# Output projection of a transformer layer as seven half-size products, with weight sums made in DRAM during attention

## The chip, the cores and the metric

The kernel runs on one core of one Trainium2 chip. The core has five engines that work from queues of their own: TensorE (PE: matmuls and transposes), VectorE (DVE), ScalarE (ACT), GpSimd (POOL) and SyncE (SP, which here only issues transfers). POOL issues transfers too, among them the ones that add to what stands at their destination. The metric is the device time of one execution in microseconds (us), the median of several.

## The reference

One layer of a streaming encoder for 512 tokens of 1024 channels, all in fp32:

```python
h = rms_norm(x, mix_norm_pre)
xa, ga, q, k, v, f_logit, g_a, g_b = split(h @ w_in)
y_a = gelu(ga) * rg_lru(causal_dwconv(xa))          # recurrent branch
y_b = forgetting_attention(q, k, v, f_logit)        # 16 heads
merged = sigmoid(g_a) * (y_a @ w_proj_a) + sigmoid(g_b) * (y_b @ w_proj_b)
mix_out = merged @ w_out                            # the output projection, 512x1024 by 1024x1024
x = x + rms_norm(mix_out, mix_norm_post)
h = rms_norm(x, ffn_norm_pre)
up = causal_dwconv(h @ w_up)                        # 1024 -> 6144
x = x + rms_norm((gelu(gate) * val) @ w_down, ffn_norm_post)
```

The change concerns `merged @ w_out` and what stands on both sides of it.

## The kernel before

**Arithmetic.** Every fp32 matrix is parted into a high and a low piece of the type fp32r, and a product is three matmuls: high by high, high by low, low by high. A weight block arrives by an SP transfer in a buffer `raw`; ACT casts it to the high piece `wh` (L172) and DVE subtracts to get the low piece `wl` (L175). Class `Split` does this, in buffers that rotate, four of each kind. The list `order` names all weight blocks in the order of use, and `unit(name, ahead)` stages the next blocks of the list before it hands out the one wanted.

**The order of the work.** A scheduler in the framework fixes one instruction order for each engine when the kernel is built; on the chip each engine goes through its order and waits on semaphores. So an instruction that waits holds up all behind it on its engine.

**Stages around the change.** After the recurrent branch come the projections for q, k and the gate `ma` with the attention of one head pair behind the next (about 280 to 440 us). Then for each of 8 output blocks e a gate projection `mb` and the projection `pb` of the attention's output `yb`; DVE multiplies gate and projection (L820), POOL adds the other branch (L821), ACT and DVE part the result into `mh` and `ml`, [128, 8, 512] each: the merged activations, channels on partitions.

**The output projection** (`out_matmuls` L832 to L840, `out_phase` L978 to L990). The 512 tokens are four tiles of 128. Phase 0 makes tiles 0 and 1, phase 1 tiles 2 and 3, each with all eight blocks of 128 rows of `w_out`, so `w_out` is read and parted twice (16 loads). A phase is 8 blocks by 2 tiles by 2 halves of 512 columns by 3 matmuls, 96 in all, 192 for both. In the last two blocks of a phase the matmuls are sorted by token tile.

**The norm of a tile** (`mix_norm`, L952 to L976). From the product in PSUM: ACT squares and sums (L957), DVE multiplies by the gain (L958), then a square root on ACT and a reciprocal on DVE (L233, L235), DVE adds the result to x (L965), ACT squares that (L967), a second root, DVE makes the normed tile `xn` (L973), PE transposes it (16 transposes, L257), ACT writes `h2h` and the copy `hf` (L261, L263), DVE writes `h2l` (L262). The norms of tiles 0 and 1 run during phase 1, with their transposes behind blocks 3 and 4 of that phase. The norms of tiles 2 and 3 run while the first six up-products use tokens 0 to 255 only (`first_half`).

**Sums in the background.** The down projection at the kernel's end is done with seven half-size products already; its sums of weight quarters `td` are made in DRAM by transfers that POOL issues, some of them adding (`down_sums` L124 to L142, `background` L147). `background(n, w)` lets POOL copy one element of a weight block that has just been staged (a tick) and issues n transfers behind it.

Of the kernel before, what the change touches and what calls it, by code (L numbers as in the profile page):

```python
# [8 lines left out]
F32 = mybir.dt.float32  # L9
# [7 lines left out]
P = 128  # L17
S = 512
# [45 lines left out]
def kernel(  # L64
# [54 lines left out]
    td = [[tdram.tile([P, D], F32, name=f"td{i}_{m}") for m in range(NS)] for i in range(4)]  # L119
# [4 lines left out]
    def down_sums():  # L124
# [7 lines left out]
        for m in range(NS + 3):  # L132
            if m < NS:
                for t, (i, c) in enumerate(((0, 0), (1, 1), (0, 1), (1, 0))):
                    yield put(t, m, down_block(i, c, m))
            if 0 <= m - 1 < NS:
                yield add(0, m - 1, down_block(0, 1, m - 1))
                yield add(2, m - 1, down_block(1, 1, m - 1))
            if 0 <= m - 2 < NS:
                yield add(1, m - 2, td[0][m - 2])  # L140
            if 0 <= m - 3 < NS:
                yield add(3, m - 3, td[1][m - 3])  # L142

    transfers = down_sums()
    tick = cpool.tile([P, 1], F32, name="tick")

    def background(n, w):  # L147
# [6 lines left out]
    class Split:  # L154


        def __init__(self, src, shape, name, pl=None):
# [4 lines left out]
            pl = pl or wpool  # L162
            self.raw = wpool.tile([P, n], F32, tag="raw", name=f"raw_{name}", padded_shape=[P, 1024])
# [7 lines left out]
        def hi(self):  # L171
            act.copy(self.wh, self.raw)  # L172

        def lo(self, engine):
            engine.tensor_tensor(out=self.wl, in0=self.raw, in1=self.wh.bitcast(F32), op=ALU.subtract)  # L175
# [7 lines left out]
    def rows(w, k):  # L183
        return w[k * P : (k + 1) * P, :], (D,)
# [14 lines left out]
    for ph in range(2):  # L199
        order += [(f"wo{ph}_{k}", *rows(w_out, k)) for k in range(KD)]  # L200
# [463 lines left out]
    def gate_tile(e, which):  # L664
        c = 0 if which == "ma" else KD
        pg = bank(f"{which}{e}")
        project(pg, unit(f"{which}{e}"), hh, hl)
# [4 lines left out]
    with ExitStack() as at:  # L672
# [108 lines left out]
        for p in range(KD):  # L781
            bias = prep_alloc(p)
            pq, pk = bank(f"q{p}"), bank(f"k{p}")
            project(pq, unit(f"q{p}"), hh, hl)
            if prev is not None:
                normalise(prev)
            project(pk, unit(f"k{p}"), hh, hl)
# [18 lines left out]
    h2h = h2pool.tile([P, KD, S], F32R, name="h2h")  # L806
    h2l = h2pool.tile([P, KD, S], F32R, name="h2l")
    offset(gstk, 448, "right")
    mgpool = gstk.enter_context(tc.tile_pool(name="merged", bufs=1, side="right", reuse_waits="tile"))
    mh = mgpool.tile([P, KD, S], F32R, name="mh")  # L810
    ml = mgpool.tile([P, KD, S], F32R, name="ml")
    for e in range(KD):
# [4 lines left out]
        for k in range(KD):  # L817
# [3 lines left out]
        pool.tensor_tensor(out=tg, in0=tg, in1=pa[:, e], op=ALU.add)  # L821
        act.activation(out=mh[:, e], in_=tg, func=AF.Copy, scale=0.5)
        dve.scalar_tensor_tensor(out=ml[:, e], in0=tg, scalar=0.5, in1=mh[:, e].bitcast(F32),
                                 op0=ALU.mult, op1=ALU.subtract)
# [7 lines left out]
    def out_matmuls(acc, toks, k, ah, al, wh, wl, nk, halves=(0, 1)):  # L832
        for t in toks:
            tok = slice(t * P, (t + 1) * P)
            for hf in halves:
                c = slice(512 * hf, 512 * hf + 512)
                dst = acc[t][hf]
                pe.matmul(dst, ah[:, tok], wh[:, c], start=k == 0, stop=False)  # L838
                pe.matmul(dst, ah[:, tok], wl[:, c], start=False, stop=False)
                pe.matmul(dst, al[:, tok], wh[:, c], start=False, stop=k == nk - 1)  # L840

    KH, SH = KD // 2, S // 2

    def sub(out, a, b):
        dve.tensor_tensor(out=out, in0=a, in1=b, op=ALU.subtract)  # L845

    A, B = slice(0, 512), slice(512, 1024)
    X, Y = slice(0, SH), slice(SH, S)
# [94 lines left out]
    with ExitStack() as mix:  # L943
# [8 lines left out]
        def mix_norm(t, acc):  # L952
            u = npool.tile([P, D], F32, tag="u", name=f"u{t}")
            xn = npool.tile([P, D], F32, tag="xn", name=f"xn2_{t}")
            s2 = small.tile([P, 2], F32, tag="s2", name=f"s2_mix{t}")
# [546 lines left out]
```

## Time and profile before

| what | value |
| --- | --- |
| median of three runs | 928.02 us (927.01, 928.02, 928.88) |
| the profiled execution: its own time | 926.11 us |
| the profiled execution: its span | 924.2 us |
| PE busy | 911.7 us of the span, 99% |
| output projection, first matmul to first up-product | 517.58 to 562.99 us |
| packets of all transfers | 182.29 MB |

The span runs from the first to the last instruction; the execution's own time is 1.9 us longer. In rows of the timeline the columns are start, duration, engine, line and operation with output and inputs, and in brackets the idle time before it and what ended that. In rows of the windows they are the stretch, its length, then busy time and count for PE, PE's weight loads, DVE, ACT and POOL, then the granted clock of PE, the share of the transfer engines and GB/s. In rows of the chain of waits they are start, time on the chain and the step. Rows of transfers end with the median time from issue to landing.

### The profile page before, as it was taken

The page shows a single profiled execution, that of the slowest core. Times are in us where ns is not written, and L with a number is a line of the kernel's source. Part 1 is how long each engine was busy: PE and PEld are TensorE (multiplying, and loading weights), DVE is VectorE, ACT ScalarE, POOL GpSimd, SP SyncE. Part 2 cuts the span into 40 slices and gives each one's busy share as a digit, 9 for nine tenths or more (in the row PEclk, how much of TensorE's full clock was granted, in tenths as well). Part 3 has the DMA queues.
Part 4 walks back from the last instruction along what each step waited for, and adds up shares of the span by engine and source line. Part 5 has one row for each costly group of instructions (what it writes and reads, how often), then busy time and mean ns, then how long its engine had stood idle before and what let it go on. Part 6 is the DMA issues. An engine that isn't in the chain of part 4 may idle for free.

```text
span 924.2 us, 14992 instructions
## 1 busy us (share of the span) xinstructions
PE 911.7 (99%) x5582; PEld 796.1 (86%) x5582; DVE 685.2 (74%) x1121; ACT 568.8 (62%) x982; POOL 230.6 (25%) x240
## 2 busy tenths in 40 slices
PE   8999999999999999999999999999999999999996
PEld 7988888887888888888888889999999999978885
DVE  5866369632857777777644588999999999889897
ACT  7555495433345566666423376688888888676664
POOL 4134345444242232220111000042323323100001
PEclk9999999999999999999999999999999999999998
DMA  7677589989776566553232755188898888799764
GB/s 278 216 227 208 165 207 256 270 211 253 176 229 152 160 148 157 151 150 86 69 114 91 271 182 163 34 212 235 218 238 204 234 208 211 223 372 325 240 201 142
DMA packets 76282, 182.29 MB, mean 197 GB/s; under 512 B 7281, under 2 KB 35745, under 8 KB 75826
## 3 DMA queue, kind: packets, MB, share of 16 engines
q1 hardware_dynamic: 45056, 123.13, 39.5%
q0 software_dynamic: 30864, 57.68, 30.2%
q8 instruction: 44, 0.72, 0.3%
q10 hardware_dynamic: 290, 0.53, 0.1%
q14 instruction: 28, 0.23, 0.1%
HBM read 148.59 MB, written 33.64 MB: 197 GB/s over the span
## 4 chain that ended last, share of the span: by engine, by line
PE 94%; DVE 2%; DMA 1%; issue 1%; ACT 0%; POOL 0%; SPq 0%; DVEq 0%; POOLq 0%
PE up L924 7%; PE up L922 7%; PE up L921 7%; PE dn L1225 4%; PE dn L1224 4%; PE dn L1223 4%; PE pa L223 2%; PE ga L224 2%; PE ga L223 2%; PE pa L224 2%; PE pa L222 2%; PE ga L222 2%; PE q L222 2%; PE ma L222 2%; PE wo L838 2%; PE mb L222 2%
## 5 line engine op out<-in xcount | busy, mean ns | idle before, releaser
L868 POOL DMA_DIRECT2D ml<-raw_up x41 | 35.0, 855 | 154.8 <-ACT ml L867 79.2
L1076 DVE SCALAR_TENSOR_TENSOR u<-up,cpt,u 128x511 f32<-128x511 f32 x96 | 71.2, 745 | 2.6 <-ACT u L1070 0.9
L1225 PE MATMUL dn<-wh_dn,al 128*128 128x512 f32 x168 | 65.6, 391 | 0.9 <-DVE al L845 0.8
L1224 PE MATMUL dn<-wl_dn,ah 128*128 128x512 f32 x168 | 65.4, 389 | 0.0
L1223 PE MATMUL dn<-wh_dn,ah 128*128 128x512 f32 x168 | 65.4, 389 | 0.0
L921 PE MATMUL up<-sh,th 128*128 128x256 f32 x252 | 60.4, 277 | 0.5 <-ACT x L928 0.5
L922 PE MATMUL up<-sl,th 128*128 128x256 f32 x252 | 60.2, 276 | 0.0
L175 DVE TENSOR_TENSOR wl_dn<-raw_dn,wh_dn 128x1024 fp32r<-128x1024 f32 x42 | 51.5, 1226 | 9.1 <-ACT wh_dn L172 9.1
L172 ACT CAST wh_dn<-raw_dn 128x1024 fp32r<-128x1024 f32 x42 | 44.1, 1050 | 17.5 <-issue 10.3
L845 DVE TENSOR_TENSOR tl<-t,th 128x1024 fp32r<-128x1024 f32 x42 | 51.1, 1218 | 1.3 <-ACT th L902 1.3
L1084 POOL TENSOR_TENSOR yf<-u,u 128x512 f32<-128x512 f32 x24 | 32.0, 1333 | 71.8 <-issue 47.5
L1070 ACT ACTIVATE u<-up,cpt 128x512 f32<-128x512 f32 x48 | 36.9, 778 | 19.8 <-PE up L924 11.0
L921 PEld LDWEIGHTS up<-sh,th 128*128 128x128 f32 x252 | 47.3, 188 | 0.7 <-ACT x L928 0.7
L922 PEld LDWEIGHTS up<-sl,th 128*128 128x128 f32 x252 | 47.3, 188 | 0.0
L902 ACT CAST th<-t 128x1024 fp32r<-128x1024 f32 x42 | 43.9, 1045 | 4.5 <-DVE t L845 1.8
L689 POOL DMA_DIRECT2D B<-maskf x32 | 39.1, 1628 | 27.2 <-DMA B<-cnd 24.1
L922 PE MATMUL up<-h2l,mh 128*128 128x256 f32 x168 | 40.2, 276 | 0.0
L921 PE MATMUL up<-h2h,mh 128*128 128x256 f32 x168 | 40.2, 276 | 0.0
L924 PE MATMUL up<-sh,tl 128*128 128x256 f32 x252 | 38.8, 276 | 0.0
L1225 PEld LDWEIGHTS dn<-wh_dn,al 128*128 128x128 f32 x168 | 31.5, 188 | 8.1 <-DVE al L845 1.7
L175 DVE TENSOR_TENSOR wl_pa<-raw_pa,wh_pa 128x640 fp32r<-128x640 f32 x16 | 13.1, 819 | 32.8 <-ACT wh_pa L172 32.8
L1224 PEld LDWEIGHTS dn<-wl_dn,ah 128*128 128x128 f32 x168 | 31.5, 188 | 6.6
(654 smaller groups left out, 3167.7 us busy)
## 6 DMA issues: line engine op xcount, KB each, us to landing
raw_up<-in_w_up_dram SPq DMA_DIRECT2D x48, 512.0 KB, 5.4
td<-in_w_down_dram POOLq DMA_DIRECT2D x36, 512.0 KB, 5.9
raw_dn<-td SPq DMA_DIRECT2D x24, 512.0 KB, 5.0
B<-cnd POOLq DMA_DIRECT2D x16, 640.0 KB, 4.8
ml<-raw_up POOLq DMA_DIRECT2D x20, 512.0 KB, 5.3
raw_dn<-in_w_down_dram SPq DMA_DIRECT2D x18, 512.0 KB, 3.5
raw_wo<-in_w_out_dram SPq DMA_DIRECT2D x16, 512.0 KB, 3.8
td<-td POOLq DMA_DIRECT2D x12, 512.0 KB, 10.8
```

What stands on the lines that cost most here:

```text
L172: act.copy(self.wh, self.raw)
L175: engine.tensor_tensor(out=self.wl, in0=self.raw, in1=self.wh.bitcast(F32), op=ALU.subtract)
L222: pe.matmul(dst, ah, bh, start=first, stop=False)
L845: dve.tensor_tensor(out=out, in0=a, in1=b, op=ALU.subtract)
L902: act.copy(self.th[i], self.t[i])
L921: pe.matmul(dst, wh[:, k], ah[:, k], start=first and k == 0, stop=False, skip_group_check=True)
L922: pe.matmul(dst, wh[:, k], al[:, k], start=False, stop=False, skip_group_check=True)
L924: pe.matmul(dst, wl[:, k], ah[:, k], start=False, stop=k == KH - 1, skip_group_check=True)
L1076: dve.scalar_tensor_tensor(out=c[:, s:], in0=ps[:, : S - s], scalar=col(C_CFW + 3 * e + j), in1=c[:, s:], op0=ALU.mult, op1=ALU.add)
L1223: pe.matmul(dst[t], ah[:, k, tok], wh[:, k], start=first, stop=False, skip_group_check=True)
L1224: pe.matmul(dst[t], ah[:, k, tok], wl[:, k], start=False, stop=False, skip_group_check=True)
L1225: pe.matmul(dst[t], al[:, k, tok], wh[:, k], start=False, stop=last, skip_group_check=True)
```

## The change

The output projection becomes seven products of half size. `w_out` is cut into four quarters (512 by 512), the merged activations into four quarters by channel half and token half (X: tiles 0 and 1, Y: tiles 2 and 3), and products of sums of quarters are added up. Each product is 2 steps (m = 0, 1) of 12 matmuls: 14 steps, 168 matmuls of 512 columns. The steps are in the order of products 1, 4, 5, 6, 7, 3, 2.

The sums of weight quarters `tw` are made by 16 transfers (8 that put, 8 that add), one behind a tick after each q, k and `ma` projection from p = 3 on, and after each `mb`. Six blocks (products 2, 3 and 7) are loaded and parted once more ahead: `cut` entries in the last six rounds of the `pb` loop; POOL writes their high and low pieces to DRAM, and SP reads the ready pieces back when the step's turn comes (L180), so those steps need no cast and no subtraction. The sums of activations are made in `merge` (L860): four POOL operations on 128x256, parted by ACT and DVE.

Products 1, 4 and 5 are copied out of PSUM by ACT (`hold`), and later products that share an accumulator (slots) are added by DVE (`fold`, L1013), with ACT squaring (L1017) and POOL multiplying by the gain (L1018). Tiles 0 and 1 are complete after step 9 (product 7); tiles 2 and 3 after product 2, whose last steps are sorted by tile. The table `then` sets which of hold, fold and norm comes behind which step.

The core of the diff (the same quarter sums serve the down projection, as before):

```diff
+    def quarter_sums(td, block, n):
...
+    transfers = quarter_sums(td, down_block, NS)
+    wo_transfers = quarter_sums(tw, out_block, NW)
+    PRODUCTS = (1, 4, 5, 6, 7, 3, 2)
+    WQ = {1: (0, 0), 2: (1, 0), 3: (1, 1), 4: 3, 5: 0, 6: 1, 7: 2}
+    OUT = [(n, m) for n in PRODUCTS for m in range(NW)]
...
+            self.split = isinstance(src, tuple)
+            if self.split:
+                self.wh = pl.tile([P, n], F32R, tag="wh", name=f"wh_{name}")
+                self.wl = pl.tile([P, n], F32R, tag="wl", name=f"wl_{name}")
+                for t, part in zip((self.wh, self.wl), src):
+                    nc.sync.dma_start(t.bitcast(F32), part)
+                return
...
+    AHEAD = [(n, m) for n in (2, 3, 7, 6)[: 6 // 2] for m in range(NW)]
...
-    for ph in range(2):
-        order += [(f"wo{ph}_{k}", *rows(w_out, k)) for k in range(KD)]
+        if e >= KD - len(AHEAD):
+            n, m = AHEAD[e - KD + len(AHEAD)]
+            order.append((f"cut{n}_{m}", out_quarter(n, m), (2, 512)))
+            cut[n, m] = [tdram.tile([P, D], F32, name=f"cut{n}_{m}_{x}") for x in "hl"]
+    order += [(f"wo{n}_{m}", tuple(cut[n, m]) if (n, m) in cut else out_quarter(n, m), (2, 512)) for n, m in OUT]
...
+    def merge(e, tg):
...
+        pool.tensor_tensor(out=tg, in0=tg, in1=pa[:, e], op=ALU.add)
+        parted(m2h[:, i], m2l[:, i], tg)
+        pool.tensor_tensor(out=raw[:, 0], in0=tg[:, X], in1=f[:, X], op=ALU.subtract)
+        pool.tensor_tensor(out=raw[:, 3], in0=raw[:, 0], in1=f[:, Y], op=ALU.add)
+        pool.tensor_tensor(out=raw[:, 1], in0=raw[:, 3], in1=tg[:, X], op=ALU.subtract)
+        pool.tensor_tensor(out=raw[:, 2], in0=raw[:, 3], in1=tg[:, Y], op=ALU.subtract)
+        for c, scale in ((slice(0, 2), 0.5), (slice(3, 4), -0.5), (slice(2, 3), 0.5)):
+            parted(qh[:, c, i], ql[:, c, i], raw[:, c], scale)
...
+        if f"cut{e}" in cut_at:
+            n, m = cut_at[f"cut{e}"]
+            parts = unit(f"cut{n}_{m}")
+            for t, part in zip(cut[n, m], parts):
+                nc.gpsimd.dma_start(t, part.bitcast(F32).rearrange("p a b -> p (a b)"))
...
+        def hold(t, h, ps):
+            act.copy(us[t][:, HALVES[h]], ps)
+
+        def fold(t, h, ps):
+            c = us[t][:, HALVES[h]]
+            dve.tensor_tensor(out=c, in0=ps, in1=c, op=ALU.add)
...
+            act.activation(out=xns[t][:, HALVES[h]], in_=c, func=AF.Square, accum_out=s2s[t][:, h : h + 1])
+            pool.tensor_tensor(out=c, in0=c, in1=gb[0][:, HALVES[h]], op=ALU.mult)
...
+        then = {
+            1: [lambda: (hold(2, 0, slot[1][0]), hold(3, 0, slot[1][1]))],
+            3: [lambda: (hold(0, 0, slot[4][0]), hold(1, 0, slot[4][1]))],
+            5: [lambda: (hold(0, 1, slot[5][0]), hold(1, 1, slot[5][1]))],
+            7: [lambda: (hold(2, 1, slot[1][0]), hold(3, 1, slot[1][1]))],
+            9: [lambda t=t, h=h: fold(t, h, slot[1][t]) for t in range(2) for h in (1, 0)] + [lambda: go(0)],
+            10: [lambda: go(1), lambda: go(0)],
+            11: [lambda: go(1)] + [lambda t=t: fold(2 + t, 1, slot[5][t]) for t in range(2)],
+        }
+        late = []
+        for i, (n, m) in enumerate(OUT):
+            w = unit(f"wo{n}_{m}", 3)
+            if i < len(OUT) - NW:
+                out_step(i, w)
+            else:
+                late.append((i, w))
+            for f in then.get(i, ()):
+                f()
...
+        for t in range(2):
+            for args in late:
+                out_step(*args, (t,))
+            go(t)
+        for t in range(2):
+            fold(2 + t, 0, slot[2][t])
```

What the scheduler makes of this is seen at three places.

**PE at the transposes of tiles 0 and 1.** Before, the transposes of tile 0 (`tr_f_0_*`, from the normed tile `xn2_0`) stand behind block 3 of phase 1:

```order
L838 MATMUL wo3_1_5254<-wh_wo1_3_5310,mh_4630 128x512
L839 MATMUL wo3_1_5254<-wl_wo1_3_5311,mh_4630 128x512
L840 MATMUL wo3_1_5254<-wh_wo1_3_5310,ml_4631 128x512
L257 MATMUL tr_f_0_0_5379<-ident_72,xn2_0_5256 128x64
L257 MATMUL tr_f_0_1_5380<-ident_72,xn2_0_5256 128x64
```

After them come the other transposes of tile 0, 12 matmuls of `wo`, the 16 transposes of tile 1, and 36 more matmuls of `wo` ahead of the first up-product. After the change, at the same tile (`wo2_0` and `wo2_1` are here the accumulators of product 2 for tiles 2 and 3):

```order
L1054 MATMUL wo2_0_5561<-wh_wo2_1_5476,m2h_4687 128x512
L1055 MATMUL wo2_0_5561<-wl_wo2_1_5477,m2h_4687 128x512
L1056 MATMUL wo2_0_5561<-wh_wo2_1_5476,m2l_4688 128x512
L284 MATMUL tr_f_0_0_5575<-ident_72,xn2_0_5451 128x64
L284 MATMUL tr_f_0_1_5576<-ident_72,xn2_0_5451 128x64
```

and, behind the other transposes of tile 0, the 12 matmuls of `wo2_1` (one of them among the transposes) and the transposes of tile 1, the last two of which head these rows:

```order
L284 MATMUL tr_f_1_0_5611<-ident_72,xn2_1_5459 128x64
L284 MATMUL tr_f_1_1_5612<-ident_72,xn2_1_5459 128x64
L249 MATMUL up0_5657<-h2h_5559,wh_up0_5512 128x256
L249 MATMUL up24_5682<-h2h_5559,wh_up24_5548 128x256
L249 MATMUL up1_5724<-h2h_5559,wh_up1_5554 128x256
```

The transposes of tile 0 have moved to the last 12 matmuls of the projection, and those of tile 1 to its very end, directly ahead of the first up-product, which reads both.

**ACT from the first root of tile 0 to its second** (`s2_f`: squares for the second norm; `sd`: square roots). Before:

```order
L233 ACT_TABLE_LOAD
L233 ACTIVATE sd_mix0_5289<-ss_mix0_5287,epst_77 128x1
L233 ACTIVATE sd_mix1_5300<-ss_mix1_5298,epst_77 128x1
L172 CAST wh_wo1_3_5310<-raw_wo1_3_5309 128x1024
L967 ACTIVATE xn2_0_5256,s2_f0_5293<-x2t_5090 128x512 x2
L172 CAST wh_wo1_4_5344<-raw_wo1_4_5343 128x1024
L172 CAST wh_wo1_5_5362<-raw_wo1_5_5361 128x1024
L967 ACTIVATE xn2_1_5263,s2_f1_5304<-x2t_5090 128x512 x2
L233 ACTIVATE sd_f0_5329<-ss_f0_5327,epst_77 128x1
```

After:

```order
L260 ACT_TABLE_LOAD
L260 ACTIVATE sd_mix0_5467<-ss_mix0_5465,epst_77 128x1
L260 ACTIVATE sd_mix1_5494<-ss_mix1_5492,epst_77 128x1
L192 CAST wh_up1_5554<-raw_up1_5553 128x1024
L1029 ACTIVATE xn2_0_5451,s2_f0_5471<-x2t_5241 128x512 x2
L192 CAST wh_up25_5719<-raw_up25_5718 128x1024
L1029 ACTIVATE xn2_1_5459,s2_f1_5498<-x2t_5241 128x512 x2
L260 ACTIVATE sd_f0_5505<-ss_f0_5503,epst_77 128x1
```

In both, the second root of tile 0 (`sd_f0`) stands behind the squares of tile 1; three casts of weights stand in the row before, two now. On DVE after, the subtractions for the same two up weights (`wl_up1`, `wl_up25`) stand between the second sum of tile 0 (`ss_f0`) and its normed tile.

**ACT at the casts of tile 0's and tile 1's transposes.** Before:

```order
L261 CAST h2h_4621<-tr_f_0_0_5379 128x8x64
L261 CAST h2h_4621<-tr_f_0_1_5380 128x8x64
L172 CAST wh_up24_5470<-raw_up24_5469 128x1024
L263 COPY hf_5098<-tr_f_0_0_5379 128x8x64
L172 CAST wh_up1_5530<-raw_up1_5529 128x1024
L263 COPY hf_5098<-tr_f_0_1_5380 128x8x64
L261 CAST h2h_4621<-tr_f_1_0_5421 128x8x64
L261 CAST h2h_4621<-tr_f_1_1_5422 128x8x64
```

After:

```order
L288 CAST h2h_5559<-tr_f_0_0_5575 128x8x64
L1017 ACTIVATE xn2_2_5539,s2_mix2_5538<-u2_5257 128x512
L288 CAST h2h_5559<-tr_f_0_1_5576 128x8x64
L1017 ACTIVATE xn2_2_5539,s2_mix2_5538<-u2_5257 128x512
L290 COPY hf_5249<-tr_f_0_0_5575 128x8x64
L192 CAST wh_up2_5818<-raw_up2_5817 128x1024
L1017 ACTIVATE xn2_3_5544,s2_mix3_5543<-u3_5258 128x512
L290 COPY hf_5249<-tr_f_0_1_5576 128x8x64
L288 CAST h2h_5559<-tr_f_1_0_5611 128x8x64
L288 CAST h2h_5559<-tr_f_1_1_5612 128x8x64
```

Between the first cast of tile 0 and the first of tile 1 now stand also three squarings for tiles 2 and 3. The last of them writes into the buffer that tile 1's normed values leave (two buffers take turns), so it waits for the transposes of tile 1.

On SP the six pairs of read-backs (`wh_wo7_0`, `wl_wo7_0` and so on) are queued in the order of use behind the load of `raw_up25`, and the next load of an up weight, `raw_up2`, behind them.

More of the change, by code (lines that the diff above doesn't have):

```diff
@@ new lines, with go @@
+        g = {}
+        def go(t):
+            if t not in g:
+                g[t] = mix_norm(t)
+            next(g[t], None)
+        then = {
[7 more added lines that the diff above has]
+        }
@@ new lines @@
+        late = []
[7 more added lines that the diff above has]
+                f()
+        h2h, h2l = [h2pool.tile([P, KD, S], F32R, tag=f"h2{x}", name=f"h2{x}") for x in "hl"]
+        for t in range(2):
[4 more added lines that the diff above has]
+            fold(2 + t, 0, slot[2][t])
```

158 lines of the change are left out of this document (83 added, 75 removed).

## The prediction

> **What bounds the kernel now.** I read the page's share by engine and its chain first, then the windows around the output projection, then PE's, ACT's and DVE's timelines there.
>
> ```profile
> span 924.2 us, 14992 instructions
> PE 911.7 (99%) x5582; PEld 796.1 (86%) x5582; DVE 685.2 (74%) x1121; ACT 568.8 (62%) x982; POOL 230.6 (25%) x240
> PE 94%; DVE 2%; DMA 1%; issue 1%; ACT 0%; POOL 0%; SPq 0%; DVEq 0%; POOLq 0%
> 517.60:563.00 45.40, 45.40 (x227) 37.19 (x226) 35.01 (x47) 31.40 (x53) 1.28 (x1) 1.00 0.71 235
> ```
>
> PE is busy 99% of the span and holds 94% of the chain that ended last. In the window of the projection it is busy all 45.40 us, ACT 31.40 and DVE 35.01. So fewer matmuls shorten the kernel by their own time, as long as PE still has something to do whenever the others are late. All of the argument lies there.
>
> What one matmul costs is the distance of starts, not the duration shown:
>
> ```profile
> L838 PE MATMUL wo<-wh_wo,mh x64: 389/389/498, 517.6 to 562.1; 128*128 128x512 f32 x64
> 517.58 0.39 PE L838 MATMUL wo<-wh_wo,mh 128*128 128x512 f32 x1
> 517.80 0.39 PE L839 MATMUL wo<-wl_wo,mh 128*128 128x512 f32 x1
> 562.76 0.23 PE wo L840
> 562.99 0.12 PE up L222
> 550.38 0.64 PE tr_f L257 x16
> ```
>
> The duration is 389 ns, but the chain puts 0.23 us on a matmul, 0.227 by the timeline's starts. 192 of them are 43.5 us; with 16 transposes twice (0.64 each) that is 44.8 of the 45.4 us from 517.58 to 562.99. The other 0.6 are small gaps, mostly around transposes.
>
> **The change, part by part.** I set T = 0 at the first product matmul; a step of 12 matmuls is 2.72 us.
>
> *Products.* 192 matmuls become 168: 24 x 0.227 = 5.4 us less. This is all that the change can save, since PE otherwise has the same rows.
>
> *The norm of tiles 0 and 1.* This decides. Before, its chain reads:
>
> ```profile
> 536.13 0.60 ACT L957 ACTIVATE xn<-wo 128x512 f32<-128x512 f32 x1 [0.98 <-PE wo L840]
> 540.19 0.20 ACT L957 ACTIVATION_READ_ACCUMULATOR xn<-wo 128x1 f32 x1
> 540.40 1.28 ACT L233 ACT_TABLE_LOAD   x1
> 541.70 0.48 ACT L233 ACTIVATE sd_mix<-ss_mix,epst 128x1 f32<-128x1 f32 x2
> 542.09 1.04 ACT L172 CAST wh_wo<-raw_wo 128x1024 fp32r<-128x1024 f32 x1
> 547.49 0.28 ACT L233 ACTIVATE sd_f<-ss_f,epst 128x1 f32<-128x1 f32 x1
> 548.61 1.41 DVE L973 SCALAR_TENSOR_TENSOR xn<-x2t,rs_f,gain 128x512 f32<-128x512 f32 x2
> 550.31 0.71 PE L257 MATMUL tr_f<-ident,xn 64*128 64x64 f32 x16
> 566.34 1.41 DVE L965 SCALAR_TENSOR_TENSOR x2t<-u,rs_mix,x2t 128x512 f32<-128x512 f32 x2
> 569.31 1.41 DVE L973 SCALAR_TENSOR_TENSOR xn<-x2t,rs_f,gain 128x512 f32<-128x512 f32 x2
> ```
>
> Tile 0's first squaring starts at 536.13, when PE has just ended the tile, and its normed tile is whole at 548.61 + 1.41 = 550.02: 13.9 us later. PE spent them on phase 1 and never waited. After the change tile 0 is whole when the first half of step 9 ends, T = 9.5 x 2.72 = 25.9. What PE has left before it reaches tile 0's transposes is the half step of tile 1, steps 10 and 11, and the last two steps of tile 2: 1.36 + 5.44 + 2.72 = 9.5 us, to T = 35.4. A chain of 13.9 us doesn't fit in 9.5; at that length PE waits 4.4 us.
>
> The new chain is not quite the old one, so I add it up in the order of the instructions, with these prices:
>
> ```profile
> 563.94 1.28 DVE L958 TENSOR_TENSOR u<-wo,gain 128x512 f32<-128x512 f32 x2
> 543.07 0.64 ACT L967 ACTIVATE xn<-x2t 128x512 f32<-128x512 f32 x1
> 565.21 1.20 DVE L175 TENSOR_TENSOR wl_up<-raw_up,wh_up 128x1024 fp32r<-128x1024 f32 x1
> 518.61 1.28 POOL L821 TENSOR_TENSOR tg_mb<-tg_mb,pa 128x512 f32<-128x512 f32 x1 [9.60 <-DVE tg_mb L820]
> ```
>
> Four DVE adds (0.64 each, half of the 1.28 for two) end at 28.7, the four squarings behind them at 29.7, the table load (1.28) at 31.0, both roots at 31.5. POOL's gains of tile 0 (2 x 1.28) are done by 29.3, those of tile 1 by 31.9, ahead of their use. x of tile 0: 31.5 to 32.9; ACT meanwhile casts an up weight (1.04), squares tile 0 (to 33.9) and casts another (to 34.95). DVE gives x of tile 1 at 35.0, so ACT's squares of tile 1 end at 36.4 and the second root of tile 0, behind them, at 36.7. DVE's subtractions for the two up weights (35.8 to 37.0, 37.15 to 38.35) are ahead of the normed tile, which is then made 38.35 to 39.7. The first half serves half of the transposes from 39.05. Wait of PE: 39.05 - 35.4 = **3.7 us**. Ends: 2.5 (one subtraction of 1.20 late enough to slip behind) and 4.4 (the old chain).
>
> *The second wait.* PE runs tile 3's last matmuls and tile 1's transposes until T = 43.25. The first up-product reads tokens 0 to 255, so it needs ACT's casts of tile 1.
>
> ```profile
> 536.63 0.19 ACT L957 ACTIVATION_READ_ACCUMULATOR xn<-wo 128x1 f32 x1
> 557.23 1.07 ACT L261 CAST h2h<-tr_f 128x512 fp32r<-128x512 f32 x2
> 558.58 0.59 ACT L263 COPY hf<-tr_f 128x512 f32<-128x512 f32 x1 [0.27 <-DVE h2l L262]
> ```
>
> At least one squaring for tile 3 (0.69 with its accumulator, less overlap), one copy (0.5) and both casts (1.07) must follow tile 1's transposes, for that squaring uses the buffer that they read: 2.3 us. By ACT's queue from tile 0's transposes (40.1) on, two casts, two squarings, a copy and a weight's cast bring it to 44.0 before that squaring, so the casts end at 46.3: a wait of 3.1 us. I take **3.1**, ends 2.3 and 4.2 (one more weight's cast ahead).
>
> *Sum without the clock.* 38.1 + 1.3 + 3.7 + 3.1, and 0.5 of small gaps, are 46.7 us where before stand 45.4: +1.3 us. Tiles 2 and 3 are folded up to 9 us ahead of the first up-product and PE reaches their transposes as before; nothing is gained there, since PE doesn't wait there now.
>
> *PE's clock.* The trace shows once what an idle PE does, at its end:
>
> ```profile
> 916.12 0.39 PE L1225 MATMUL dn<-wh_dn,al 128*128 128x512 f32 x1
> 918.00:918.50 0.50, 0.00 (x0) 0.00 (x0) 0.50 (x1) 0.05 (x1) 0.25 (x1) 1.00 0.93 369
> 918.50:919.00 0.50, 0.00 (x0) 0.00 (x0) 0.42 (x2) 0.04 (x1) 0.00 (x0) 0.80 0.94 361
> 919.00:919.50 0.50, 0.00 (x0) 0.00 (x0) 0.18 (x2) 0.25 (x1) 0.00 (x0) 0.50 0.78 303
> ```
>
> The last matmul ends at 916.5; the granted clock goes from 1.00 to 0.50 at 918.8 (0.80 in that half microsecond), 2.3 us later. My first wait is 3.7 us, so I count on it to halve. How soon it comes back no row shows: between at once and the whole 3.36 us of work up to the second wait done at half speed, 0 to 3.4 us more. Taking the middle, 1.7, tile 1's transposes end at 45.0, and of the lateness 1.0 us reaches the up-products, because ACT was itself only free at 44.0. Should the clock be low after the second wait too, up to 1.7 us more; I count 0.3. Together **+1.3**. The Trainium skill ("TensorE: Matmul & The Clock Gate", Part 1: The HAM clock gate) has the clock halve after an idle window of about 3.4 us that runs freely, and come back after about 3.4 us of work. The 2.3 us of the trace is shorter than that window, and the measurement decides; by the page the first wait would only sometimes hold a whole idle window, and that case is priced as the second rival.
>
> *What I cost at nothing.* The 16 sum transfers and their ticks:
>
> ```profile
> 360.00:440.00 80.00, 80.00 (x544) 66.97 (x543) 57.30 (x154) 48.95 (x119) 18.11 (x18) 1.00 0.51 135
> 440.00:517.60 77.60, 77.60 (x349) 64.53 (x348) 37.45 (x38) 24.96 (x36) 8.98 (x7) 1.00 0.33 106
> 444.27 1.05 ACT L172 CAST wh_mb<-raw_mb 128x1024 fp32r<-128x1024 f32 x1 [2.77 <-PE mb L223]
> 446.94 0.28 PE pb L222
> 448.31 0.62 ACT L777 CAST yb<-y 128x512 fp32r<-128x512 f32 x1 [0.76 <-DVE y L775]
> td<-td POOLq DMA_DIRECT2D x12, 512.0 KB, 10.8
> ml<-raw_up POOLq DMA_DIRECT2D x20, 512.0 KB, 5.3
> ```
>
> POOL has 18 of 80 us to do there and the transfer engines are half idle; without that cover a weight would come late by one such transfer, 5 to 11 us once. In the `pb` rounds (second row: ACT 25, DVE 37, POOL 9 of 77.6 us) the four POOL operations, the partings and the cut blocks fit beside PE. One edge: the cast of a gate block (444.27) now waits for POOL's write of a cut block, issued about one cast later (445.4, an estimate) and landed after up to 5.3 us, at 450.7; behind it stand the two pieces of `yb` (some 2.4 us with the gate's cast), and PE wants them 21 matmuls into its first row of `pb`, at 446.94 + 4.8 = 451.7. That is 0 to 1.4 us; I take 0, since the landing is the median of adding transfers and this one only writes. `hold` copies end before their slots are wanted again; if not, 0.6 us each.
>
> *Read-backs.* Six pairs of 512 KB, in SP's queue behind `raw_up25`, from T = 13.6 on.
>
> ```profile
> 830.00:860.00 30.00, 30.00 (x134) 24.86 (x133) 28.16 (x36) 20.75 (x29) 0.00 (x0) 1.00 0.94 326
> 597.00:640.00 43.00, 41.63 (x363) 41.24 (x363) 41.38 (x59) 37.92 (x58) 15.53 (x15) 1.00 0.88 220
> ```
>
> At 326 / 0.94 = 347 GB/s a pair takes 3.0 us, a little over a step; with 3.3 us for the first to land, the last lands near T = 35, wanted at 34.2 at the latest, and the first wait takes up such lateness. At 220 / 0.88 = 250 GB/s see the third rival.
>
> Total: +1.3 + 1.3 = +2.6 us, 928.7 for the profiled execution (926.1), whose time is 1.9 us under the median of the runs shown; against that median of 928.0 it is **930.6 us**. Differences under 0.2% (1.9 us) can't be told from no change.
>
> **The rivals.**
>
> 1. *The norm fits under its cover; not slower.* The old chain held three weight casts between its roots, the new one two, and the chain's own parts are short: where tile 2 ran undisturbed, it was 4.4 us from the start of x (566.34) to the end of the normed tile (569.31 + 1.41), and adds, squares, table and root are about 5. If the chain of tile 0 takes under 9.5 us, the first wait is gone, the clock stays, and the second is 0 to 3: -5.4 to -2 us, about 924.5. For it: ACT and DVE have fewer weights to part now. Against it: one ACT row carries both tiles, and the second root of tile 0 comes behind tile 1's squares.
> 2. *The clock stays up.* Both waits as forecast, but the clock doesn't halve in 3.7 us, or comes back at once: +1.3, 929.3, within what can't be told apart. It decides whether the 2.3 us at the trace's end are a delay that always holds or one chance of several; one instance is all there is. By the window that the Trainium skill gives on the page named above this would be the usual case.
> 3. *Read-backs late.* At 250 GB/s a pair takes 4.2 us, the last lands at T = 13.6 + 2 + 25 = 40.8, 6.6 us late; the first wait covers 3.7 of it, so 2.9 are added: 933. For it: that row has background transfers beside SP's; against: none are queued here.
>
> That the matmuls aren't saved I leave out: PE's order has 24 rows fewer.
>
> **How the numbers follow.** Forecast 0.40 (+1.3 to +4.5, mostly above 0.2%), rival 1 0.20 (mostly below), rival 2 0.25 (mostly within), rival 3 0.15 (above). Faster: most of rival 1, 0.17. Same: 0.05 of rival 1, 0.20 of rival 2, 0.07 of the forecast, 0.32. Slower: the rest, 0.51. The range leaves out the better half of rival 1 (0.12) and the far end of rival 3 (0.07): 926.0 to 934.0.
>
> **What would show it.** In the changed profile, PE should have idle time ahead of the transposes of tile 0 of about 3.7 us, released by DVE's `xn`, and about 3 us ahead of the first up-product, released by ACT's `h2h`; the stage from the first product to the first up-product should last about 47 to 48 us; the granted clock should dip below 1.00 in it. No idle time ahead of tile 0's transposes makes me wrong on the main step; idle time there released by a transfer means the third rival.

## The result, and the profile after

The changed kernel takes 937.85 us (median of four runs, 937.01 to 942.19), the kernel before on the same chip 928.12 us (927.01 to 928.88). The ratio is 1.0113, 95% interval 1.0095 to 1.0131: slower by 9.7 us, where +2.6 was forecast and 934 was the end of the range. The profiled execution took 937.01 us, its span 11.0 us more than the span of before.

The page's first rows:

```profile
span 935.2 us, 15107 instructions
PE 911.7 (97%) x5558; PEld 793.4 (85%) x5558; DVE 684.9 (73%) x1131; ACT 575.4 (62%) x1001; POOL 290.2 (31%) x315
```

The window from the first product to the first up-product:

```profile
517.80:571.80 54.00, 44.18 (x202) 33.64 (x201) 32.84 (x49) 30.42 (x60) 14.71 (x12) 0.94 0.78 292
```

PE, busy for all of this stage before, is idle for 10 of its 54 us, and the mean clock is 0.94. By the starts of the matmuls, the stage before the projection ends 0.26 us later than in before (517.84 against 517.58), the projection takes 53.94 us (before 45.25: +8.7), and the stage from the first up-product to the first down-product 238.5 (before 236.35: +2.1). Those three are the 11.0 us. The sum transfers, the ticks and the cut blocks during attention cost nothing that can be seen.

PE's waits from 515 to 600 us (total us, times, longest):

```profile
PE tr_f L284 <- DVE xn L1035: 3.6, 1, 3.6
PE up L249 <- ACT h2h L288: 2.3, 1, 2.3
PE wo L1054 <- DMA wh_wo<-cut_h: 1.8, 1, 1.8
PE wo L1055 <- DMA wl_wo<-cut_l: 1.1, 2, 0.8
PE wo L1055 <- DVE wl_wo L196: 0.9, 2, 0.8
```

The first two rows are the two forecast waits, the other three weights that come late. Where they lie, in PE's timeline:

```profile
530.24 0.50 PE L1055 MATMUL wo<-wl_wo,qh 128*128 128x512 f32 x1 [0.75 <-DVE wl_wo L196]
543.58 0.47 PE L1054 MATMUL wo<-wh_wo,qh 128*128 128x512 f32 x1 [1.82 <-DMA wh_wo<-cut_h]
544.89 0.50 PE L1055 MATMUL wo<-wl_wo,qh 128*128 128x512 f32 x1 [0.85 <-DMA wl_wo<-cut_l]
557.76 0.50 PE L1055 MATMUL wo<-wl_wo,m2h 128*128 128x512 f32 x1 [0.21 <-DMA wl_wo<-cut_l]
562.78 0.69 PE L284 MATMUL tr_f<-ident,xn 64*128 64x64 f32 x8 [3.60 <-DVE xn L1035]
```

The first late weight is the first block of product 5. Its cast stands on ACT behind the last partings of `merge`, which wait for POOL; DVE's subtraction follows:

```profile
525.87 0.42 ACT L855 ACTIVATE qh<-sums 128x256 fp32r<-128x256 f32 x1 [1.36 <-POOL sums L871]
527.90 1.03 ACT L192 CAST wh_wo<-raw_wo 128x1024 fp32r<-128x1024 f32 x1
528.96 1.23 DVE L196 TENSOR_TENSOR wl_wo<-raw_wo,wh_wo 128x1024 fp32r<-128x1024 f32 x1 [0.52 <-ACT wh_wo L192]
```

The piece is whole at 530.19 and PE goes on at 530.24. SP's queue hangs on it too. SP's timeline, a row of DVE's, and a row of SP's waits from 515 to 565 us:

```profile
530.21 7.61 SPq L185 DMA_DIRECT2D raw_up<-in_w_up_dram  x4
538.01 0.33 SPq L180 DMA_DIRECT2D wh_wo<-cut_h  x1
536.25 1.23 DVE L196 TENSOR_TENSOR wl_up<-raw_up,wh_up 128x1024 fp32r<-128x1024 f32 x1 [0.69 <-ACT wh_up L192]
SPq L185 <- DVE wl_up L196: 1.5, 1, 1.5
```

The issue of the four loads of up weights is spread over 7.6 us, since each needs a `raw` buffer that a weight must leave first. The first is issued at 530.21, as product 5's first block is subtracted (530.19), the second and third behind the next two blocks of `wo` (532.10 and 535.56). The fourth, directly ahead of the read-backs, takes the buffer of the first of these loads: that weight has to land, to be cast on ACT (from 535.16) and to be subtracted on DVE (until 537.48) before it. So the first read-back is issued only at 538.01, T = 20.2. PE waits for it from 541.76 to 543.58, 5.6 us after its issue. The page's rows of transfers give the median of all six (last column, us to landing):

```profile
wh_wo<-cut_h SPq DMA_DIRECT2D x6, 512.0 KB, 7.8
wl_wo<-cut_l SPq DMA_DIRECT2D x6, 512.0 KB, 7.6
```

Last the clock, in windows:

```profile
560.50:561.00 0.50, 0.00 (x0) 0.00 (x0) 0.50 (x4) 0.04 (x1) 0.00 (x0) 0.74 0.00 0
565.00:566.00 1.00, 1.00 (x3) 0.81 (x4) 0.91 (x2) 1.00 (x4) 0.00 (x0) 0.50 0.59 234
```

And two rows of the chain of waits:

```profile
565.96 0.43 PE wo L1054
568.15 0.23 PE wo L1054
```

The granted clock is at half from 560.74 to 567.56, and a matmul takes 0.43 us of the chain there instead of 0.23. PE worked again from 562.78, so 4.8 us of work were done at half speed: 2.4 us.

The stage in sum: products -5.45, late weights +5.6 (1.4 at 530, 0.5 at 538, 3.2 at 541 to 545, 0.5 at 557), first wait +3.8, second wait +2.5, half clock +2.4: +8.8, measured +8.7.

### The profile page after: what moved, and what is told of

It is laid out like the page before. It is cut to its first block, busy times and chain, and to the rows that moved or that the text cites. A ratio compares the mean times of both kernels' runs of the same rounds, so it can differ in the third digit from the quotient of the medians.

```text
span 935.2 us, 15107 instructions
## 1 busy us (share of the span) xinstructions
PE 911.7 (97%) x5558; PEld 793.4 (85%) x5558; DVE 684.9 (73%) x1131; ACT 575.4 (62%) x1001; POOL 290.2 (31%) x315
## 5 line engine op out<-in xcount | busy, mean ns | idle before, releaser
L719 POOL DMA_DIRECT2D B<-maskf x32 | 43.0, 1795 | 27.0 <-DMA B<-cnd 23.8
L754 ACT ACTIVATE P<-P,mx 128x384 f32<-128x384 f32 (+3 forms) x64 | 35.3, 552 | 3.0 <-DVE mx L749 1.9
```

Of the source, the lines that this page charges most:

```text
L719: nc.gpsimd.dma_start(diag, mask2, accum_op=ALU.add)
```

## The experiments

The theory after the result: three causes of like size, late weights (5.6), the two waits of the norm (6.2), and the half clock that the waits bring (2.4). The rival: one cause underlies the others, and taking it away gives the gain of 5.4. Every run below stands beside runs of the kernel before on the same chip (927.0, 927.2 and 927.4 us median in the three groups). Stage lengths are from one profile each, by starts of matmuls; that of the version with tiles 2 and 3 in turn is of its longest execution (931.35 us, median 928.01). The fourth column has the stretches of PE's clock at half, in us, without the one at the kernel's end.

| kernel | projection | up stage | half clock ahead of the end | time | ratio to before (95%) |
| --- | --- | --- | --- | --- | --- |
| before | 45.25 | 236.35 | none | 928.12 | |
| changed | 53.94 | 238.48 | 6.8 us | 937.85 | 1.0113 (1.0095 to 1.0131) |
| no cut blocks | 51.91 | 241.45 | 10.2 + 6.8 | 938.94 | 1.0116 (1.0098 to 1.0135) |
| first wait filled | 53.76 | 241.30 | 3.4 + 6.8 | 939.88 | 1.0133 (1.0116 to 1.0149) |
| both waits filled | 51.66 | 244.22 | 3.4 + 3.4 | 940.56 | 1.0140 (1.0126 to 1.0154) |
| read-backs ahead on SP | 49.07 | 241.72 | 3.4 + 6.8 | 936.32 | 1.0093 (1.0078 to 1.0108) |
| norm rearranged | 51.29 | 238.50 | 3.4 + 3.4 | 933.63 | 1.0070 (1.0046 to 1.0094) |
| norm rearranged, second way | 47.48 | 238.94 | none | 932.91 | 1.0066 (1.0051 to 1.0082) |
| all repairs | 42.26 | 241.19 | none | 928.64 | 1.0012 (1.0001 to 1.0022) |
| all repairs, two cut products | 44.76 | 242.31 | 3.4 | 932.57 | 1.0055 (1.0043 to 1.0068) |
| all repairs, tiles 2 and 3 in turn | 42.74 | 241.25 | 3.4 | 928.01 | 1.0004 (0.9994 to 1.0014) |
| the same, gains of tiles 2 and 3 on POOL | 42.62 | 240.63 | none | 928.34 | 1.0009 (0.9998 to 1.0020) |

**No cut blocks.** All fourteen blocks are cast and parted when their turn comes, so that there are no read-backs.

```diff
-    AHEAD = [(n, m) for n in (2, 3, 7, 6)[: 6 // 2] for m in range(NW)]
+    AHEAD = [(n, m) for n in (2, 3, 7, 6)[:0] for m in range(NW)]
```

> No block is cut ahead: products 7, 3 and 2 load their raw weights (6 x 512 KB instead of 12) and part them on ACT and DVE like the others; nothing is written out in the last rounds of pb. Theory (the weights come late because read-backs stand behind the up loads in SP's queue and land late): the 4.1 us that PE lost on read-backs and most of the 1.3 us lost later in the up stage go, while the wait for the normed tile stays at 3.5 to 5 us, since casts of w_out now stand in the norm's chain; about 4 to 5 us faster than the changed kernel, 933. Rival (the norm's chain sets the end whatever the weights do): PE then reaches the transposes earlier and waits as much longer; 936 to 938.

938.94 us, not faster, where the theory had 933. No weight is late any more, but PE's waits, in the same view, are now:

```profile
PE tr_f L284 <- DVE xn L1035: 7.1, 1, 7.1
PE up L249 <- ACT h2h L288: 2.3, 1, 2.3
```

The chain of tile 0 takes longer, since ACT and DVE part six blocks more in this stage: from its first addition on DVE at 545.83 to its normed tile at 562.2 it is 16.4 us, against 549.16 to 563.4, 14.2, in the changed kernel. Part of that is DVE beside POOL's four multiplications (548.16 to 555.23): a weight's subtraction took 2.31 us there, elsewhere 1.2, and the two additions of 128x1, elsewhere 0.15, took 1.25 and 1.24. The 3.2 us of late read-backs come back as 3.5 us more at the first wait, with a longer half clock. The cut blocks do what they are for.

**The waits filled.** To separate the clock from the waits, unused matmuls (their outputs are overwritten) keep PE busy: 17 ahead of tile 0's transposes, and in a second kernel 12 more ahead of the first up-product.

```diff
+    FILL = 17
...
+        for _ in range(FILL if name == "f" and t == 0 else 0):
+            pe.matmul(tbs[0], m2h[:, 0, :P], m2h[:, 1], start=True, stop=True)
```

```diff
+            for _ in range(12 if e == 0 else 0):
+                pe.matmul(first[0][0], first[0][1][0][:, 0], first[0][1][0][:, :4], start=True, stop=True)
```

> The changed kernel with 17 more matmuls (17 x 0.227 = 3.9 us) of unused data ahead of the transposes of tile 0, where PE waits 3.8 us. Theory (the clock halves in that wait and costs 2.5 us): the granted clock stays at 1.00 there, the transposes and the 12 matmuls behind take 3.9 us instead of 6.5, of which up to 1 us is given back in the second wait; 1.5 to 2.5 us faster than the changed kernel, 935.5 to 936.5. Rival (the clock is low for another reason, or its cost is hidden by ACT's queue ahead of the first up-product): no change within 0.5 us, 937.9.

> The fill of the run before and 12 more unused matmuls (2.7 us) ahead of the first up-product, so that PE idles in neither wait. Theory (the clock is set by windows of 3.41 us that run on their own; an idle stretch of some 2 us or more in one of them halves the clock for the next one or two, wherever that falls): no stretch at half clock behind tile 0's transposes, the up stage takes 238 us as in the changed kernel and not 241.3; 936 to 937. Rival (filling itself costs what it saves, or the half clock has another cause): 939 to 941, as with the first fill alone.

939.88 and 940.56 us: the first is above what either of its expectations had, the second is where its rival had it. With the first wait filled, the clock stayed at 1.00 over that stretch and up to the second wait. Two windows of that kernel, one over the filled stretch, one behind the second wait:

```profile
555.00:563.00 8.00, 8.00 (x36) 6.32 (x34) 8.00 (x13) 4.79 (x12) 1.22 (x1) 1.00 0.46 176
571.00:572.00 1.00, 1.00 (x4) 0.80 (x4) 1.00 (x1) 1.00 (x4) 1.00 (x2) 0.50 0.00 0
```

So the idle time does halve the clock. But nothing was gained: the clock now halved at the wait for read-backs (543.43 to 546.84) and behind the second wait (570.74 to 577.56). With that one filled as well, the first up-product no longer waited for `h2h`, and PE waited as long one step on, for DVE. Its waits:

```profile
PE wo L1057 <- DMA wh_wo<-cut_h: 2.9, 1, 2.9
PE up L251 <- DVE h2l L292: 2.3, 1, 2.3
```

and the clock halved behind both, from 545.60 to 549.01 and from 576.32 to 579.73. The up stage took 244.2 us, where the theory had 238. The two kernels also got another order on DVE and ACT, so their times don't price the clock alone; what they show is that the clock halves at other waits, of 1.6 to 2.9 us, when this one is gone.

**Read-backs ahead of the up loads.** On SP the loads of `up1` and `up25` go behind the read-backs.

```diff
+    behind = []
...
-                    nc.sync.dma_start(t.bitcast(F32), part)
+                    behind[:] = [nc.sync.dma_start(t.bitcast(F32), part)]
...
-            nc.sync.dma_start(self.raw, src)
+            with ExitStack() as put:
+                if name in ("up1", f"up{JF + 1}"):
+                    for i in behind:
+                        put.enter_context(tc.issue_after(i.ins))
+                nc.sync.dma_start(self.raw, src)
```

> Only SP's order is changed: the loads of up weights 1 and 25 stand behind the read-backs, not ahead. Theory: the first read-back is issued at about 534 instead of 538.0 (it then waits only for its buffer), the 4.1 us that PE lost on read-backs fall to under 1.5, and the two casts leave the norm's chain, whose wait falls by 1 to 2 us; 4 to 5 us faster than the changed kernel, 933 to 934. Rival (the transfer engines are full, so that the read-backs land 8 us after issue whenever they are issued, or later still): PE's loss on read-backs stays above 2.5 us; 935 to 937.

PE's waits in this kernel:

```profile
PE tr_f L290 <- DVE xn L1041: 2.8, 1, 2.8
PE up L255 <- ACT h2h L294: 2.3, 1, 2.3
PE up L256 <- DVE h2l L295: 1.2, 1, 1.2
PE wo L1061 <- DVE wl_wo L202: 0.8, 1, 0.8
PE wo L1060 <- ACT wh_wo L198: 0.7, 1, 0.7
```

No wait for `cut_h` or `cut_l` is left, though product 5's first block still comes late, by 1.9 us: the lateness was the place in SP's queue, not a limit of what the transfers can move. So the time, 936.32 us, lies in the rival's range, but its sign, over 2.5 us lost on read-backs, did not come. The projection is 4.9 us shorter (0.8 of it by a shorter first wait), the total only 1.5, with intervals that overlap. The clock now is at half from 568.14 to 574.97, across the first up-products, and the up stage takes 3.2 more; in this profile the projection also begins 1.3 us later.

**The norm rearranged.** ACT's table load goes ahead of the squares (behind the last `hold`), tile 1's transposes ahead of its last matmuls on PE, so that the 6 last matmuls cover the casts, the load of `up1` with its cast and subtraction behind the norm, and the additions of tiles 2 and 3 behind the transposes. In the first kernel DVE multiplies by the gain for tiles 0 and 1 only and the tiles go one after the other; in the second DVE multiplies all four, in `mix_norm`, and tiles 0 and 1 go in turn. The second:

```diff
-            pool.tensor_tensor(out=c, in0=c, in1=gb[0][:, HALVES[h]], op=ALU.mult)
...
+            for c in HALVES:
+                dve.tensor_tensor(out=u[:, c], in0=u[:, c], in1=gb[0][:, c], op=ALU.mult)
...
+            7: [lambda: (hold(2, 1, slot[1][0]), preload(hold(3, 1, slot[1][1])))],
+            9: [lambda t=t, h=h: fold(t, h, slot[1][t]) for t in range(2) for h in (1, 0)]
+            + [lambda t=t: go(t) for t in (0, 1, 0, 1)],
...
+            act.activation(out=tick, in_=epst, func=AF.Sqrt)
...
+            for args in late:
+                out_step(*args, (0,))
+            go(0)
+            with tc.issue_after(marks["tr"].ins):
+                out_step(*late[0], (1,))
+            go(1)
+            with tc.issue_after(marks["tr"].ins):
+                out_step(*late[1], (1,))
+            for t in range(2):
+                fold(2 + t, 1, slot[5][t])
+                fold(2 + t, 0, slot[2][t])
```

> Only the norm of tiles 0 and 1 is rearranged: tile 0 first, the table for the root loaded ahead, gain by DVE for these tiles, the up weights 1 and 25 staged behind the chain, the transposes of tile 1 ahead of the last 6 matmuls of product 2. Theory: the wait for tile 0's normed values (3.8 us), the second wait (2.5) and the half clock (2.5) go to under 1 us each, the 5.6 us of late weights stay; 6 to 8 us faster than the changed kernel, 930 to 932. Rival (transfers are the bound: read-backs land late and everything behind them moves with them): under 3 us faster, 935 or more.

> Only the norm part of the repair. Theory (two separate losses, the weights 5.6 us and the norm with the clock about 6 to 8): the wait ahead of tile 0's transposes under 0.5 us, that ahead of the first up-product under 0.5, the late weights as in the changed kernel; 930 to 932. Rival (each loss hides behind the other, so that neither repair alone brings more than half): 934 or more.

933.63 and 932.91 us: 4 to 5 us better than the changed kernel, so the norm's waits and the half clock behind them are about half of the loss; both times lie between the two expectations. In the first kernel 3.1 us of waiting for `xn` were left. Its group of normed halves (least, median and greatest ns):

```profile
L1036 DVE SCALAR_TENSOR_TENSOR xn<-x2t,rs_f,gain x8: 742/749/1754, 558.1 to 581.6; 128x512 f32<-128x512 f32 x8
```

and DVE's and POOL's timelines there:

```profile
563.35 2.41 DVE L1036 SCALAR_TENSOR_TENSOR xn<-x2t,rs_f,gain 128x512 f32<-128x512 f32 x2
565.69 1.22 DVE L1024 TENSOR_TENSOR ss_mix<-s_mix 128x1 f32<-128x1 f32 x1
563.40 3.49 POOL L1019 TENSOR_TENSOR u<-u,gain 128x512 f32<-128x512 f32 x2 [35.08 <-ACT xn L1018]
```

Half of a normed tile took 1754 ns instead of 742 while POOL multiplied, an addition of 128x1 1.22 us. In the second kernel the gains are on DVE and the clock never halves. In the projection late weights are all that is left there of size: 1.1 + 1.0 us at 530, 2.4 + 1.0 at 543.

**All repairs.** The second norm, the read-backs ahead on SP, and the cast of product 5's first block ahead of the last `merge`:

```diff
+        with ExitStack() as hold_back:
+            if e == KD - 1:
+                fetch(where["wo5_0"])
+                hold_back.enter_context(tc.issue_after(casts["wo5_0"].ins))
+            merge(e, tg)
```

> All suspected causes mended in one kernel, with the seven products kept: the norm of tiles 0 and 1 in its shortest order and with the gain on DVE, the table ahead, tile 1's transposes ahead of the last 6 matmuls, up weights 1 and 25 loaded behind the read-backs, the weights of product 5 parted ahead of the last merge. Theory (late weights, the norm's cover and the half clock are the whole loss): under 2 us of waits left in the stage, which lasts 40 to 42 us, no half clock, 1 to 2 us more in the up stage than before the change; 924 to 926, faster than the kernel before by 1 to 3 us. Rival (the added transfers fill the transfer engines and something always comes late): stage above 44 us, 928 or more.

928.64 us, as the rival had it, but without its sign, a stage above 44 us. The projection takes 42.26 us, 3.0 less than before the change: the 5.4 of the products less 2.1 of waits and 0.4 of small gaps. Against the norm alone this is 5.2 us off the projection and 4.3 us off the time; that is what the late weights cost. But the up stage takes 4.8 us more than before, and the total is no shorter. PE's waits from 515 to 600 us:

```profile
PE tr_f L291 <- DVE xn L1047: 1.8, 3, 1.1
PE up L257 <- DVE h2l L296: 0.4, 1, 0.4
PE up L256 <- ACT h2h L295: 0.4, 1, 0.4
```

The same with only products 2 and 3 cut, so that product 7's blocks are cast in their turn:

```diff
-    AHEAD = [(n, m) for n in (2, 3, 7, 6)[: 6 // 2] for m in range(NW)]
+    AHEAD = [(n, m) for n in (2, 3, 7, 6)[: 4 // 2] for m in range(NW)]
```

> The repaired kernel with only products 2 and 3 cut ahead (4 blocks, not 6), product 7 parted on ACT and DVE where they are idle. Theory: within 1 us of the repaired kernel. Rival (transfers are the bound): 1.5 us or more faster than it, since 1 MB less is read and 1 MB less written.

932.57 us, 4 us slower, which neither expectation had. ACT stood still for an up weight's transfer, and a `hold` copy that frees an accumulator came behind it:

```profile
538.75 1.05 ACT L199 CAST wh_up<-raw_up 128x1024 fp32r<-128x1024 f32 x1 [1.82 <-DMA raw_up<-in_w_up_dram]
542.70 1.07 ACT L1019 COPY u<-wo 128x512 f32<-128x512 f32 x2
```

PE waited 2.95 us for that copy. The prediction had priced a late `hold` at 0.6.

**Tiles 2 and 3.** To win back the up stage, their norms go in turn instead of one after the other, and in a second kernel POOL multiplies them by the gain.

```diff
-        next(g2)
         fetch(where[f"up{1 + JF}"])
...
+        next(g2)
+        next(g3)
```

```diff
-                dve.tensor_tensor(out=u[:, c], in0=u[:, c], in1=gb[0][:, c], op=ALU.mult)
+                (dve if t < 2 else pool).tensor_tensor(out=u[:, c], in0=u[:, c], in1=gb[0][:, c], op=ALU.mult)
```

> The version with all four repairs, with one edit more: the norms of tiles 2 and 3 go in turn, step by step, behind the first half up-products, where tile 2 went whole ahead of tile 3. Theory (in the repaired version the output projection takes 42.3 us, 3.0 less than before the change, and what is left of the loss lies in the up stage, 241.2 us against 236.4, of which about 1.3 us are PE's wait for the transposes of tile 3): that wait goes, the up stage takes 239.5 to 240.2, 927.2 us, the same as before or just faster. Rival (DVE's queue of partings and gains sets the end of tile 3, so the order of the two tiles moves the wait from tile 3 to tile 2): up stage 241 again, 928.6. The waits for adding transfers, 2.3 us against 0.9, stay in both.

> As the version with tiles 2 and 3 in turn, with POOL instead of DVE multiplying tiles 2 and 3 by the gain (four operations of 128x512). Theory (DVE's queue of partings and gains behind the transposes of tile 1 makes the end of tiles 2 and 3 late): four times 0.64 us less on DVE, the waits ahead of the transposes of tiles 2 and 3 are under 0.5 us together, 926.5 to 927 us. Rival (POOL's and DVE's operations slow each other, as the 742 ns of a normed half that took 1754 ns beside POOL's multiplications showed): the time of tile 2 grows by about 1 us and nothing is gained or up to 1 us lost, 928 to 929.

928.01 and 928.34 us, both not to be told from before. The wait for `xn` in the up stage did not shrink in the first (1.3 us, 1.1 before this edit), and the up stage took 241.25 us, as its rival had it. In the second it was 0.4, and one for a weight's low piece came in its stead; DVE was slow beside POOL again, as that rival had it (an addition of 128x1 took 1.20 us). The second kernel's waits from 560 to 815 us:

```profile
PE up L987 <- DMA ml<-raw_up: 2.0, 2, 1.2
PE up L258 <- DVE wl_up L203: 1.1, 1, 1.1
PE up L257 <- DVE h2l L296: 0.4, 1, 0.4
PE tr_f L291 <- DVE xn L1047: 0.4, 1, 0.4
```

The first row, before:

```profile
PE up L924 <- DMA ml<-raw_up: 0.9, 1, 0.9
```

These are transfers that add to the low pieces of up weights. Of the 4.3 us that this kernel's up stage has more than before's, the rows give 3.0 (1.1 by the adding transfers, 1.9 behind the norm). The other 1.3 us are spread thinly over the stage and stay open, as does why the adding transfers come later; neither was tried. No version beat the kernel before.

## Why the prediction was wrong, point by point

- **Products, -5.4:** right, -5.45.
- **First wait, 3.7:** right, 3.8, with the chain as I added it up: 13.15 us from tile 0's first addition to half of its normed tile in the sum, 13.5 measured (549.16 to 562.65), with both up weights' subtractions ahead of the normed tile. That the sum fits so well is in part luck. x of tile 0, which I priced at 1.4 us, took 2.49, as it began beside POOL's last multiplication, which I took as free; the other parts were some 0.7 us shorter than priced.

```profile
554.52 2.49 DVE L1027 SCALAR_TENSOR_TENSOR x2t<-u,rs_mix,x2t 128x512 f32<-128x512 f32 x2
550.74 5.06 POOL L1018 TENSOR_TENSOR u<-u,gain 128x512 f32<-128x512 f32 x4 [23.20 <-ACT xn L1017]
```

- **Second wait, 3.1:** right within its ends, 2.5. The chain's last part, in ACT's timeline, is as told: a squaring for tile 3, a copy, the casts.

```profile
569.56 0.63 ACT L1017 ACTIVATE xn<-u 128x512 f32<-128x512 f32 x1 [0.99 <-PE tr_f L284]
570.65 1.07 ACT L288 CAST h2h<-tr_f 128x512 fp32r<-128x512 f32 x2
```

- **Read-backs, costed at nothing "from T = 13.6 on": the step that failed.** The first was issued at T = 20.2. The prediction gives the 13.6 without working, and lets the loads ahead start freely, though each `raw_up` waits for a rotating buffer: the first three for blocks of products 5 and 6, the fourth for the first of these same loads, which must land and be parted before. So the lateness of product 5's first block went on to the first load, from it to the fourth, and to the read-backs behind that. Its own lateness, 1.4 us behind the partings of `merge`, was not in the sum at all. And I priced a landing at 3.3 us, while PE got the first piece 5.6 us after its issue and the median is 7.8 with several under way. Together 5.6 us; taking all of it away, on top of the rearranged norm, brought 5.2 us off the projection, and moving the read-backs alone 4.9, with 1.9 us left at product 5 and a shorter first wait. Nor did "the first wait takes up such lateness" hold: a late product delays the start of tile 0's chain by as much as PE's arrival, so the waits add up. The third rival named the effect with another mechanism (rate, 2.9 us) and half its size.
- **The clock, +1.3:** right in kind, 2.4 in size by the account of the stage (no run prices it alone), inside the ends that I gave (0 to 3.4). The second rival falls: a wait of 3.8 us halved it.
- **The first rival** (the norm fits under its cover) falls: the chain took 13.5 us; its cover, 9.5 in the prediction, was 9.9 (549.16 to 559.02).
- **What lies behind the projection** I took as unchanged. It was 2.1 us longer, and 4.3 to 6.0 with the projection repaired. Of the 2.1, 1.2 are waits for the transfers that add to low pieces of up weights (2.1 us, 0.9 before). With the projection repaired, what ACT and DVE no longer do under PE's waits they owe in the up stage. That this is why tile 3 and the first up weights come late there is argued from the order; the runs show only that the one stage's gain was the other's loss.

The sum had the stage 2.6 us longer, measured are 8.7. Of the 6.1 missing, 5.6 are the late weights, 1.1 the clock and 0.1 the first wait, less 0.6 of the second, to within small gaps. The 2.1 of the up stage and 0.26 of what lies ahead make the rest.

## What to carry to other kernels

A transfer priced at nothing needs its issue time, and that comes from the whole chain of buffers ahead of it on its queue: ask for each load which buffer it needs, who frees that and behind what this stands. The one that frees it may be a load a few places ahead on the same queue. When PE loses work, the cover for the norm and for staged weights shrinks by the same time; here 5.4 us saved had to be paid with waits of 2 to 4 us that were hidden before. Mending one wait at a time moved the loss to the next one, so judge a repair by its stage and by the stage behind it.

## What the runs showed of the hardware

- **The clock goes by fixed windows.** Ahead of the kernel's end the half-clock stretches last 3.41, 6.83 or 10.24 us: one, two or three times 3.413. So do the stretches at full speed: in the changed kernel from 11.19 to 560.74 us (161.0 times) and from 567.56 to 932.79 (107.0 times). The Trainium skill ("TensorE: Matmul & The Clock Gate", Part 1: The HAM clock gate) states this window, 3413 ns and running freely, and the runs agree. It has the clock fall after an idle window of about 3.4 us. Here windows in which PE was busy for nearly half of the time could be enough, but were not always. Of these three windows the first two are of the changed kernel, the third of that with the first wait filled:

```profile
540.26:543.67 3.41, 1.59 (x8) 1.02 (x6) 0.00 (x0) 1.17 (x2) 0.00 (x0) 1.00 1.00 323
557.33:560.74 3.41, 1.64 (x6) 0.86 (x5) 3.41 (x7) 2.80 (x8) 0.00 (x0) 1.00 0.50 204
540.02:543.43 3.41, 1.62 (x7) 0.79 (x5) 0.00 (x0) 0.99 (x2) 0.00 (x0) 1.00 1.00 406
```

  Behind the first, the clock stayed at 1.00; behind the other two it fell to half. PE was busy for 1.59, 1.64 and 1.62 us of them, so the busy time that the profile shows does not settle when the clock falls. What does stays open, and with it why the wait for the same read-backs left the clock alone in one kernel and halved it in the other.
- **Landings under load.** 512 KB took 7.8 us (median) with several read-backs queued, while other loads of this size in the same kernel have medians from 3.6 us on.
- **DVE and POOL slow each other** when both work on 128x512 pieces in SBUF: 742 ns became 1754 while POOL took 3.49 us for two multiplications (2.54 for two at 566.13 in the changed kernel), and x of tile 0 in the changed kernel 2.49 us instead of 1.41, in the rows above. In the repaired versions that multiply by the gain on DVE alone, this is gone from the norm.
